# Latents in one pass, their norm ahead of the token scale, and softmax planes read later in a two-layer trunk

## The chip, the cores and the metric

The kernel runs on one core of a Trainium2 chip. The time is device microseconds of one execution. TensorE (PE in the profile) does the matrix products, ScalarE (ACT) and VectorE (DVE) the elementwise work, SyncE (SP) issues nearly all DMAs.

## The reference

Two pre-norm residual layers on 256 tokens of width 2048, fp32, 16 heads of 128. Layer a is multi-head latent attention: x is projected to a query latent (512), a key/value latent (256), one shared rotary key (64) and a gate (2048); both latents get an RMS norm of their own before they are projected up to the heads. Layer b is block attention, where 256 tokens are a single block, so it is causal attention with ALiBi. In both the output is multiplied with silu(gate) and projected back.

```python
h = rms_norm(x, g)                                   # per layer
proj = h @ w_in                                      # layer a
q_lat, kv_lat, k_rope, gate = proj[..., :512], proj[..., 512:768], proj[..., 768:832], proj[..., 832:]
q = rms_norm(q_lat) @ w_q_up;  kv = rms_norm(kv_lat) @ w_kv_up
o = causal_block_attention(q, k, v, 192 ** -0.5)     # q, k: 128 plain + 64 rotary, with QK norm
x = x + (o * silu(gate)) @ w_out_a
# layer b: q, k, v, gate from w_in_b, QK norm, ALiBi, x = x + (o * silu(gate)) @ w_out_b
```

## The kernel before

x is kept transposed (`xt`: 16 chunks of 128 features by 256 tokens). Each fp32 product is three TensorE matmuls of rounded parts: high times high, low times high, high times low. x is split by `split_x` (L331: ScalarE makes the high part, DVE the low one); a weight tile `W` is loaded by SP into `wr` (4 buffers), ScalarE makes `wh` (L147), DVE makes `wl` (L151). PSUM has 8 banks: five accumulators `acc` and three work banks.

The order of the program comes from `ordered(main, side)`: `main` is the list of matmul steps, `side` holds steps that become due some planner time after their `needs` (a step's lag, times 1.3). The result is run step by step; the matmuls are chained in that order, and each engine then works through its own instructions in the order given.

At the start, layer a's 832 latent columns are made in two passes over x, `lat0` and `lat1`, each 416 columns wide for 16 chunks. While `lat1` runs, the squares of x are summed; `token_scale` (L353) turns the sums into one factor per token: `ps_st` (a matmul with ones), three Newton rounds (`rsqrt`), and a step `g` that puts the root on a diagonal and spreads it by a matmul `ps_r`. `lat_out` copies the latents out of PSUM with that factor, `lat_norm` squares, norms and scales them; `lat_t` transposes them (`ps_lt`), for which TensorE has one and a half gate blocks (`gates[0]`, `gates[1][:HALF]`) to do meanwhile.

Then come eight groups of two heads (`group_a`): q_up and kv_up, then `turn`, and for each head `head_steps` (L450): s1 scores and softmax, s2 turns the probabilities by a DMA transpose between two byte-plane copies (`fly` on ScalarE and SP, then a copy of `pz` on DVE, L448) and splits them in `ph` (ScalarE) and `pl` (DVE, L491); s3 multiplies with v (`ps_o`) and writes `ohl`, the gated output. Between them stand the gate blocks.

The output projection `outs_a` has eight blocks of 256 columns. `out_done_a` adds a finished block to `xt`, splits it for layer b and sums its squares. A `reload` step brings `xt` back and at last the ALiBi table into `c_sb`; the first `alibi` bias (L883, ScalarE) reads it. The last projection `outs_b` ends with an add and a DMA to `outT` (L922).

## Time and profile before

| | |
|---|---|
| median of 3 runs | 754.15 us (752.91 to 754.26) |
| profiled execution | 752.38 us, span 750.6 us, mean TensorE clock 0.999 of full |
| TensorE busy | 740.6 us (99%) |
| DVE busy | 589.5 us (79%) |
| ScalarE busy | 491.3 us (65%) |
| DMA | 71.6% of 16 engines' span on SP's queue |

Busy is the time in which the engine has an instruction under way. Matmuls overlap in their pipeline, so an engine can be shown busy while a later one starts late; the distance from one start to the next says more. The bracket behind a timeline row tells the idle time in front of the instruction and what ended it.

### The profile page before, as it was taken

Reading aid. Unit: us, or ns where it says so; the run is one execution under the profiler, and the core shown is the slowest. Engines: PE = TensorE matmul, PEld = TensorE weight load, DVE = VectorE, ACT = ScalarE, POOL = GpSimd, SP = SyncE. Lnnn points to the kernel's source line nnn. Section 1 sums busy time; section 2 is a strip of 40 time slices with the busy share of each in tenths; the row PEclk is TensorE's granted clock in tenths of the full one; section 3 lists DMA queues with packets and bytes.
Section 4 is the critical chain, followed back from the end, with each engine's and each line's share of the span. In section 5 each row is a group of like instructions: output and inputs, shape, how many; then the busy total and the mean of one; then the engine's idle time right before and its main releaser. Section 6 shows DMA issues by size and latency. Waiting matters only on the chain.

```text
span 750.6 us, 13198 instructions
## 1 busy us (share of the span) xinstructions
PE 740.6 (99%) x4766; PEld 689.4 (92%) x4766; DVE 589.5 (79%) x1244; ACT 491.3 (65%) x1041; POOL 0.2 (0%) x4
## 2 busy tenths in 40 slices
PE   8999999999999999999999999999999999999997
PEld 7999999999999989988889988898889988899997
DVE  6978899999998696775788867887787967878563
ACT  7767888888877575555666666675666766565441
POOL 0000000000000000000000000000000000000000
PEclk9999999999999999999999999999999999999999
DMA  9866666666666966667787868877779778867761
GB/s 301 268 177 183 169 185 162 180 177 153 189 180 180 294 196 221 198 181 210 222 223 210 205 197 225 230 201 205 208 227 220 200 212 223 215 214 201 249 221 49
DMA packets 150258, 153.13 MB, mean 204 GB/s; under 512 B 47280, under 2 KB 119344, under 8 KB 150192
## 3 DMA queue, kind: packets, MB, share of 16 engines
q1 hardware_dynamic: 150048, 152.27, 71.6%
q8 instruction: 37, 0.61, 0.3%
q14 instruction: 29, 0.24, 0.1%
q10 hardware_dynamic: 144, 0.02, 0.0%
HBM read 139.68 MB, written 2.10 MB: 189 GB/s over the span
## 4 chain that ended last, share of the span: by engine, by line
PE 90%; DVE 5%; DMA 2%; ACT 1%; issue 1%; SPq 0%; DVEq 0%; ACTq 0%
PE acc L199 83%; PE ps_s L199 4%; DVE wl L151 3%; PE ps_o L199 2%; PE ps_ta L202 1%; DMA c_sb<-cst 1%; DMA wr<-w_in_a 1%; ACT wh L147 1%; DMA sm<-pz 0%; DVE xt L406 0%; ACT sq L598 0%; ACT sf L584 0%; DVE rs_y L328 0%; DVE rs_t L327 0%; PE ps_lt L202 0%
## 5 line engine op out<-in xcount | busy, mean ns | idle before, releaser
L147 ACT ACTIVATE wh<-wr 128x1024 fp32r<-128x1024 f32 (+3 forms) x265 | 288.4, 1092 | 143.1 <-PE acc L199 116.6
L151 DVE TENSOR_TENSOR wl<-wr,wh 128x1024 fp32r<-128x1024 f32 (+3 forms) x265 | 314.1, 1189 | 72.3 <-PE acc L199 41.8
L199 PE MATMUL acc<-wh,xhl 128*128 128x512 f32 (+1 forms) x896 | 265.6, 375 | 0.9 <-ACT wh L147 0.9
L199 PEld LDWEIGHTS acc<-wh,xhl 128*128 128x128 f32 x896 | 169.0, 190 | 21.7 <-ACT wh L147 1.5
L199 PE MATMUL acc<-xhl,wh 128*128 128x256 f32 (+1 forms) x768 | 173.4, 313 | 0.0
L199 PE MATMUL acc<-ohl,wh 128*128 128x256 f32 (+1 forms) x800 | 172.2, 307 | 0.0
L199 PE MATMUL acc<-wl,xhl 128*128 128x512 f32 (+1 forms) x448 | 167.8, 375 | 0.8 <-DVE wl L151 0.8
L199 PE MATMUL acc<-ohl,wl 128*128 128x256 f32 x512 | 140.7, 275 | 0.6 <-DVE wl L151 0.6
L199 PE MATMUL acc<-xhl,wl 128*128 128x256 f32 x512 | 140.3, 274 | 0.0
L199 PEld LDWEIGHTS acc<-ohl,wh 128*128 128x128 f32 x800 | 130.1, 191 | 6.0
L199 PEld LDWEIGHTS acc<-xhl,wh 128*128 128x128 f32 x768 | 126.5, 191 | 6.5
L199 PEld LDWEIGHTS acc<-ohl,wl 128*128 128x128 f32 x512 | 98.4, 192 | 1.3 <-DVE wl L151 1.2
L199 PEld LDWEIGHTS acc<-xhl,wl 128*128 128x128 f32 x512 | 98.4, 192 | 0.2
L199 PEld LDWEIGHTS acc<-wl,xhl 128*128 128x128 f32 x448 | 85.0, 190 | 11.6 <-DVE wl L151 1.6
L199 PE MATMUL acc<-wh,xt 128*128 128x384 f32 (+1 forms) x192 | 57.3, 356 | 0.0
L466 ACT ACTIVATE sm<-sm,mn 128x128 f32<-128x128 f32 x64 | 29.1, 457 | 12.9 <-DVE mn L464 12.9
L199 PEld LDWEIGHTS acc<-wh,xt 128*128 128x128 f32 x192 | 35.1, 190 | 1.2
L199 PE MATMUL acc<-wl,xt 128*128 128x384 f32 (+1 forms) x96 | 33.6, 350 | 1.5 <-DVE wl L151 1.5
L406 DVE TENSOR_TENSOR xt<-acc,xt 128x256 f32<-128x256 f32 (+1 forms) x37 | 16.1, 484 | 14.1 <-PE acc L199 14.1
L490 ACT CAST ph<-pz 128x256 fp32r<-128x256 f32 x32 | 12.9, 403 | 18.8 <-DVE pz L483 10.6
L507 DVE TENSOR_TENSOR ohl<-og,ohl 128x256 fp32r<-128x256 f32 x32 | 13.5, 424 | 12.2 <-ACT ohl L506 11.7
L506 ACT ACTIVATE ohl<-og 128x256 fp32r<-128x256 f32 x32 | 13.8, 433 | 12.8 <-DVE og L505 12.7
(150 smaller groups left out, 724.9 us busy)
## 6 DMA issues: line engine op xcount, KB each, us to landing
wr<-w_in_b SPq DMA_DIRECT2D x128, 512.0 KB, 4.0
wr<-w_in_a SPq DMA_DIRECT2D x32, 512.0 KB, 4.1
wr<-w_out_a SPq DMA_DIRECT2D x32, 512.0 KB, 4.5
wr<-w_out_b SPq DMA_DIRECT2D x32, 512.0 KB, 4.4
wr<-w_in_a SPq DMA_DIRECT2D x15, 416.0 KB, 5.0
wr<-w_q_up SPq DMA_DIRECT2D x16, 384.0 KB, 3.8
wr<-w_kv_up SPq DMA_DIRECT2D x8, 512.0 KB, 4.0
xt<-xT SPq DMA_DIRECT2D x4, 512.0 KB, 5.2
```

The lines of the kernel that those rows point to most:

```text
L147: nc.scalar.activation(self.ordering(self.h)[1], self.ordering(self.raw)[0], AF.Copy)
L151: nc.vector.tensor_tensor(self.ordering(self.l)[1], self.ordering(self.raw)[0], self.ordering(self.h.bitcast(F32))[1], op=ALU.subtract)
L199: chain(nc.tensor.matmul(*args, skip_group_check=True, **kw))
L202: chain(nc.tensor.transpose(*args))
L406: nc.vector.tensor_tensor(lines(y), unpaired(b[:, o:o + n]), lines(y), op=ALU.add)
L466: nc.scalar.activation(sm[:, sl], sm[:, sl], AF.Exp, bias=mn[:, t:t + 1], scale=-1.0, accum_out=rs[:, t:t + 1])
L490: nc.scalar.copy(ph, pz[:, :S])
L506: nc.scalar.activation(lines(ogh[:, h]), unpaired(og), AF.Copy)
L507: nc.vector.tensor_tensor(lines(ogl[:, h]), unpaired(og), lines(ogh[:, h].bitcast(F32)), op=ALU.subtract)
```

## The change

The latents are made in one pass: for each chunk of x both halves (832 columns) are multiplied, four accumulators are held, the x tiles are loaded in other places, and wl is used as the third of three products. The squares of x are summed in that pass. `lat_squares` takes the squares of the latents directly from PSUM; the tokens' factor enters through EPS (`lat_e`), and `normed` scales straight out of PSUM, one token half on ScalarE, the other on DVE. `token_scale` is three steps, its root and diagonal in one. `head_steps` of groups 1 to 5 gets `away=FLA`: `fly` early, the copy and the split (`s2_back`, L487 after) 1.3 × 4000 planner ns later. The output blocks, one gate block of layer b and the end of the last output block are reordered.

```diff
@@ -44,8 +44,8 @@
 
 
 
-PA, PB, LO, TU, TUB, S1, S2A, S2B, S3 = 9000, 6000, 5000, 3000, 10000, 4800, 6000, 9000, 3000
-FLB = 4500
+PA, PB, LO, TU, TUB, S1, S2A, S2B, S3 = 9000, 6000, 6000, 3000, 10000, 4800, 6000, 9000, 3000
+FLA, FLB = 4000, 4500
 SLACK = 1.3
 HOLD = 4500
 PACE, PACEB = 600, 3500
@@ -356,24 +356,28 @@
         def f():
             ps = work("ps_st")
             for t in range(2):
-                matmul(ps[:, t * P:(t + 1) * P], ssq[:, t * P:(t + 1) * P], ones, start=True, stop=True)
-            v = one.tile([P, 2], F32, name="rv_" + lay)
-            nc.vector.tensor_scalar(v, ps[:, :2 * P:P], 1.0 / DM, EPS, op0=ALU.mult, op1=ALU.add)
+                matmul(ps[:, t:t + 1], ssq[:, t * P:(t + 1) * P], ones[:, :1], start=True, stop=True)
+            v = out["v"] = one.tile([P, 2], F32, name="rv_" + lay)
+            nc.vector.tensor_scalar(v, ps[:, :2], 1.0 / DM, EPS, op0=ALU.mult, op1=ALU.add)
+
+        def h():
             r = out["r"] = one.tile([P, 2], F32, name="r_" + lay)
-            nc.vector.tensor_copy(r, rsqrt(v, 2, "x"))
+            d = out["diag"] = wk.tile([P, S], F32, tag="og", name="diag")
+            with tc.high_priority():
+                nc.vector.tensor_copy(r, rsqrt(out["v"], 2, "x"))
+                for t in range(2):
+                    nc.vector.tensor_scalar(d[:, t * P:(t + 1) * P], ident, r[:, t:t + 1], None, op0=ALU.mult)
             more()
 
         def g():
             pr = work("ps_r")
-            d = wk.tile([P, S], F32, tag="og", name="diag")
-            for t in range(2):
-                nc.vector.tensor_scalar(d[:, t * P:(t + 1) * P], ident, out["r"][:, t:t + 1], None, op0=ALU.mult)
-            matmul(pr[:, :S], ones, paired(d), start=True, stop=True)
+            matmul(pr[:, :S], ones, paired(out["diag"]), start=True, stop=True)
             rows = out["rows"] = one.tile([P, S], F32, tag="rr", name="rr_" + lay)
             nc.vector.tensor_copy(rows, pr[:, :S])
 
-        a = Step(f, 436, lag, needs, bank=True)
-        return a, Step(g, 436, 1500, [a], bank=True)
+        a = Step(f, 200, 800, needs, bank=True)
+        b = Step(h, 0, lag - 800, [a])
+        return a, b, Step(g, 436, 1500, [b], bank=True)
 
 
     gate_of = {}
@@ -540,7 +544,7 @@
         return Step(f, 0, 1000)
 
     def rest():
-        with tc.issue_after(lat1[0].w.dma):
+        with tc.issue_after(latent[7].w.dma):
             nc.sync.dma_start(g_sb[:, G_QN:G_END], gains[:, G_QN:])
             nc.sync.dma_start(c_sb, cst[:, :C_COS])
 
@@ -577,38 +581,70 @@
 
     lat_acc = []
 
-    def lat_out(i):
-        def f():
-            o = i * LAT // 2
-            for t in range(2):
-                nc.scalar.activation(lat[t][:, o:o + LAT // 2], lat_acc[i][t], AF.Copy, scale=scale_a["r"][:, t:t + 1])
-            if i:
-                lat_norm()
-        return f
-
     lat_st = {}
+    hf = LAT // 2
+
+    def blk_latents():
+
+
+        def go(wt, k, js):
+            if not lat_acc:
+                lat_acc.extend([acc("acc")[:, :hf] for _ in range(2)] for _ in range(2))
+            for i, j in enumerate(js):
+                ws = slice(i * hf, (i + 1) * hf)
+                wh, wl = paired(wt.h[:, 0, ws]), paired(wt.l[:, 0, ws])
+                for x, w, first, last in ((xh, wh, True, False), (xl, wh, False, False), (xh, wl, False, True)):
+                    for t in range(2):
+                        matmul(lat_acc[j][t], x[:, k, t * P:(t + 1) * P], w,
+                               start=k == 0 and first, stop=k == NC - 1 and last)
+
+        def step(k, js):
+            wt = W(w_in_a[k * P:(k + 1) * P, js[0] * hf:(js[-1] + 1) * hf], True)
+            return Step(lambda: go(wt, k, js), 6 * len(js) * 176, 0, w=wt)
+
+        return [step(0, (0,)), step(0, (1,))] + [step(k, (0, 1)) for k in range(1, NC)]
+
+
+    segments = ((0, 0, hf, 0, 0), (1, 0, QR - hf, hf, 0), (1, QR - hf, QR + KVR - hf, QR, 1), (1, QR + KVR - hf, hf, QR + KVR, 2))
+
+    def lat_squares():
+        with tc.high_priority():
+            squares_of()
+        tables()
+
+    def squares_of():
+        st = lat_st["st"] = one.tile([P, 2, 4], F32, name="lat_st")
+        for t in range(2):
+            for i, (j, lo, hi, _, _) in enumerate(segments):
+                sq = wk.tile([P, 512], F32, tag="gx", name="sq")
+                nc.scalar.activation(sq[:, :hi - lo], lat_acc[j][t][:, lo:hi], AF.Square, accum_out=st[:, t, i:i + 1])
 
     def lat_norm():
-        st = one.tile([P, 2, 3], F32, name="lat_st")
+        with tc.high_priority():
+            normed()
+
+    def normed():
+
+
+        st = lat_st["st"]
         v = one.tile([P, 2, 3], F32, name="lat_v")
-        parts = ((0, QR), (QR, KVR), (QR + KVR, ROPE))
-        for t in range(2):
-            for i, (o, n) in enumerate(parts):
-                sq = wk.tile([P, 512], F32, tag="gx", name="sq")
-                nc.scalar.activation(sq[:, :n], lat[t][:, o:o + n], AF.Square,
-                                     accum_out=st[:, t, i:i + 1])
...
+        ev = one.tile([P, 2], F32, name="lat_e")
+        nc.vector.tensor_scalar(ev, scale_a["v"], EPS, None, op0=ALU.mult)
+        nc.vector.tensor_tensor(st[:, :, 1], st[:, :, 0], st[:, :, 1], op=ALU.add)
+        for i, n in enumerate((QR, KVR, ROPE)):
+            nc.vector.scalar_tensor_tensor(v[:, :, i], st[:, :, i + 1], 1.0 / n, ev, op0=ALU.mult, op1=ALU.add)
         r = rsqrt(v.rearrange("p a b -> p (a b)"), 6, "l")
         krz = wk.tile([P, 384], F32, tag="sm", name="krz", bufs=3).rearrange("p (t a d) -> p t a d", t=2, a=3)
         nc.vector.memset(krz, 0.0)
         rp = wk.tile([P, 2, 1, ROPE], F32, tag="rp", name="rp", bufs=1)
...
+        for j, lo, hi, at, i in segments:
+            for t in range(2):
+                out = rp[:, t, 0] if i == 2 else lat[t][:, at:at + hi - lo]
+                by = r[:, 3 * t + i:3 * t + i + 1]
+                if t == 0:
+                    nc.scalar.activation(out, lat_acc[j][t][:, lo:hi], AF.Copy, scale=by)
+                else:
+                    nc.vector.tensor_scalar(out, lat_acc[j][t][:, lo:hi], by, None, op0=ALU.mult)
...
...
@@ -733,7 +768,7 @@
         for h in range(2):
             heads.append(head_steps(2 * g + h, scores(h), lambda: c_sb[:, C_MASK:C_MASK + 384],
                                     lambda h=h: [x[:, h] for x in z["v"]], 1090, turns + [kr], [], gates[g][-1:],
-                                    S2A, nc.scalar.copy))
+                                    S2A, nc.scalar.copy, away=FLA if 0 < g < 6 else 0))
         proj[0].needs += lats
         if g > 1:
             proj[-1].after += turns_of[-2]
@@ -745,22 +780,21 @@
         return proj
 
     pieces = [(0, 1), (1, 2), (2, 4), (4, 6), (6, 8), (8, 10), (10, 12), (12, 14), (14, 16)]
-    for i, (c0, c1) in enumerate(pieces):
-        main += [x_split(c0, c1)] + lat0[c0:c1]
-        for j in ((1, 2) if i == 0 else (i + 2,)):
-            if j < len(pieces):
-                lat0[pieces[j][0]].w.before = x_load(*pieces[j])
     squares = [Step(lambda j=j: sum_squares(ssq_a, 2 * j) or sum_squares(ssq_a, 2 * j + 1), 0, 2500) for j in range(4)]
-    main += lat1[:2] + [Step(rest)]
-    for j in range(4):
-        main += [squares[j]] + lat1[2 * j + 2:2 * j + 4]
-    main += lat1[10:] + gates[0] + gates[1][:HALF]
-    col_a, row_a = token_scale(ssq_a, "a", scale_a, squares, tables)
-    lo = [Step(lat_out(i), 0, LO, [col_a], b[-1:]) for i, b in enumerate((lat0, lat1))]
-    lo[1].after.append(lo[0])
-    lats = [Step(lat_t(b), 440, 2500, lo, bank=True) for b in range(3)]
+    main += [x_split(0, 1)] + latent[:2]
+    for i, (c0, c1) in enumerate(pieces[1:]):
+        latent[c0 + 1].w.before = x_load(c0, c1)
+        main += [x_split(c0, c1)] + [squares[j] for j in range(4) if c1 == (6, 10, 14, 16)[j]] + latent[c0 + 1:c1 + 1]
+        if c1 == 6:
+            main += [Step(rest)]
+    main += gates[0] + gates[1][:HALF]
+    col_a, r_a, row_a = token_scale(ssq_a, "a", scale_a, squares, lambda: None)
+    sq = Step(lat_squares, 0, 3000, latent[-1:])
+    lo = Step(lat_norm, 0, LO, [col_a, sq])
+    lo.after.append(r_a)
+    lats = [Step(lat_t(b), 440, 2500, [lo], bank=True) for b in range(3)]
     kr = Step(kr_t, 440, 2500, lats, bank=True)
-    side += [col_a, row_a] + lo + lats + [kr]
+    side += [col_a, r_a, sq, lo, row_a] + lats + [kr]
 
     def reload(j):
         def f():
@@ -814,9 +848,8 @@
             outs_a[2 * j][-1].needs.append(again)
     for b in outs_a[:4]:
         main += b[:12]
-    for b in outs_a[:4]:
-        main += b[12:]
-    main += sum(outs_a[4:], [])
+    o = outs_a
+    main += o[0][12:] + o[4][:8] + o[1][12:] + o[4][8:] + o[2][12:] + o[5][:8] + o[3][12:] + o[5][8:] + o[6] + o[7]
 
 
     x_b = x_a
@@ -911,6 +944,8 @@
         turns_of.extend([[tq], [tk]])
         side.extend([tq, tk])
         side.extend(s for h in hb[-4:] for s in h)
+        if g == 0:
+            gate = gate[:12] + gate[NC:NC + 4] + gate[12:NC] + gate[NC + 4:]
         return gate + q + k + v
 
     def out_done_b(c0, m):
@@ -918,6 +953,12 @@
             xt = res["x"]
             for b in range(0, len(a), m):
                 c = c0 + 2 * b // m
+                if c == NC - 2:
+                    for i, queue in enumerate((nc.sync, nc.scalar)):
+                        y = xt[:, c + i]
+                        nc.vector.tensor_tensor(lines(y), unpaired(a[b][:, i * S:(i + 1) * S]), lines(y), op=ALU.add)
+                        queue.dma_start(outT[(c + i) * P:(c + i + 1) * P], y)
+                    continue
                 added(a[b:b + m], xt, c)
                 nc.sync.dma_start(outT[c * P:(c + 2) * P].rearrange("(c p) t -> p c t", p=P), xt[:, c:c + 2])
         return f
@@ -925,8 +966,8 @@
     outs_b = [(blk_both if 8 <= c < 14 else blk_cols)(w_out_b[:, c * P:(c + n) * P], og, out_done_b(c, 2 if 8 <= c < 14 else 1))
               for c, n in ((0, 4), (4, 4), (8, 2), (10, 2), (12, 2), (14, 2))]
 
-    col_b, row_b = token_scale(ssq_b, "b", scale_b, [outs_a[7][-1]], scales_b, 7500)
-    side += [col_b, row_b]
+    col_b, r_b, row_b = token_scale(ssq_b, "b", scale_b, [outs_a[7][-1]], scales_b, 7500)
+    side += [col_b, r_b, row_b]
     hb = []
     for g in range(4):
         main += group_b(g)
```

DVE's order in the second group, before. `pz`, `pl` are planes of the heads, `gx` and `gate` the gate, `sr` the turned q and k, `wl` (128x1024) kv_up:

```order
L448 COPY pz<-sm 128x2x384
L151 TENSOR_TENSOR wl<-wr,wh 128x768
L491 TENSOR_TENSOR pl<-pz,ph 128x256
L394 TENSOR_TENSOR gx<-acc,rr_a 128x512
L151 TENSOR_TENSOR wl<-wr,wh 128x768
L448 COPY pz<-sm 128x2x384
L396 SCALAR_TENSOR_TENSOR gate<-gate,gx 128x512
L491 TENSOR_TENSOR pl<-pz,ph 128x256
L427 SCALAR_TENSOR_TENSOR sr_1704<-ps_ta,gq_a,sr_1704 128x256
L427 SCALAR_TENSOR_TENSOR sr_1704<-ps_ta,g_sb,sr_1704 128x512
L427 SCALAR_TENSOR_TENSOR sr_1704<-ps_ta,sr_1704 128x128
L151 TENSOR_TENSOR wl<-wr,wh 128x1024 x2
```

The same place after:

```order
L151 TENSOR_TENSOR wl<-wr,wh 128x768
L398 TENSOR_TENSOR gx<-acc,rr_a 128x512
L151 TENSOR_TENSOR wl<-wr,wh 128x768
L400 SCALAR_TENSOR_TENSOR gate<-gate,gx 128x512
L431 SCALAR_TENSOR_TENSOR sr_1695<-ps_ta,gq_a,sr_1695 128x256
L487 COPY pz<-sm 128x2x384
L431 SCALAR_TENSOR_TENSOR sr_1695<-ps_ta,g_sb,sr_1695 128x512
L495 TENSOR_TENSOR pl<-pz,ph 128x256
L431 SCALAR_TENSOR_TENSOR sr_1695<-ps_ta,sr_1695 128x128
L151 TENSOR_TENSOR wl<-wr,wh 128x1024
L487 COPY pz<-sm 128x2x384
L151 TENSOR_TENSOR wl<-wr,wh 128x1024
```

Both copies moved behind the gate; the second, and its `pl`, moved behind the first wl of kv_up.

DVE's order at layer b's token scale, before (`rs_y`, `rs_t`: the Newton rounds; `r_b`: the root; `diag`: what TensorE's `ps_r` reads):

```order
L326 TENSOR_TENSOR rs_t<-rv_b,rs_y 128x2
L327 SCALAR_TENSOR_TENSOR rs_t<-rs_t,rs_y 128x2
L328 SCALAR_TENSOR_TENSOR rs_y<-rs_t,rs_y 128x2
L363 COPY r_b<-rs_y 128x2
L151 TENSOR_TENSOR wl<-wr,wh 128x1024
L786 TENSOR_TENSOR rx_126<-r_b 128x2
L370 TENSOR_SCALAR diag<-c_sb,r_b 128x128
L787 TENSOR_SCALAR rx_126<-rx_126 128x2
L370 TENSOR_SCALAR diag<-c_sb,r_b 128x128
```

And after:

```order
L326 TENSOR_TENSOR rs_t<-rv_b,rs_y 128x2
L151 TENSOR_TENSOR wl<-wr,wh 128x1024
L327 SCALAR_TENSOR_TENSOR rs_t<-rs_t,rs_y 128x2
L328 SCALAR_TENSOR_TENSOR rs_y<-rs_t,rs_y 128x2
L367 COPY r_b<-rs_y 128x2
L369 TENSOR_SCALAR diag<-c_sb,r_b 128x128 x2
```

The wl that stood between root and diagonal now stands inside the last Newton round; root and diagonals follow each other.

ScalarE's order at the end of layer a's heads, before (`ohl`: the last two heads' outputs; `alibi`: the first bias of layer b, which reads the `c_sb` load):

```order
L147 ACTIVATE wh<-wr 128x1024 x2
L506 ACTIVATE ohl<-og 128x256
L147 ACTIVATE wh<-wr 128x1024
L506 ACTIVATE ohl<-og 128x256
L883 ACTIVATE alibi<-c_sb 128x384
L147 ACTIVATE wh<-wr 128x1024 x2
```

And after:

```order
L147 ACTIVATE wh<-wr 128x1024 x2
L510 ACTIVATE ohl<-og 128x256
L147 ACTIVATE wh<-wr 128x1024
L916 ACTIVATE alibi<-c_sb 128x384
L510 ACTIVATE ohl<-og 128x256
L147 ACTIVATE wh<-wr 128x1024
```

`alibi` moved in front of the last head's `ohl`.

## Rows read from the trace of the kernel before

**Rows 1.** Page, parts 1 and 4: busy time by engine, and the chain.
```profile
PE 740.6 (99%) x4766; PEld 689.4 (92%) x4766; DVE 589.5 (79%) x1244; ACT 491.3 (65%) x1041; POOL 0.2 (0%) x4
...
PE 90%; DVE 5%; DMA 2%; ACT 1%; issue 1%; SPq 0%; DVEq 0%; ACTq 0%
```

**Rows 2.** Windows: length, each engine's busy time (instructions), clock, DMA share, GB/s.
```profile
0.00:10.00 10.00, 7.26 (x47) 5.96 (x47) 4.57 (x10) 6.22 (x11) 0.20 (x4) 1.00 0.79 238
10.00:20.00 10.00, 9.85 (x54) 9.52 (x55) 9.08 (x16) 9.12 (x16) 0.00 (x0) 1.00 1.05 360
250.00:260.00 10.00, 10.00 (x92) 10.00 (x92) 5.81 (x9) 2.89 (x4) 0.00 (x0) 1.00 1.06 340
260.00:280.00 20.00, 19.40 (x134) 17.85 (x133) 18.13 (x31) 15.48 (x24) 0.00 (x0) 1.00 0.58 179
340.00:390.00 50.00, 50.00 (x234) 43.85 (x233) 35.09 (x60) 29.14 (x54) 0.00 (x0) 1.00 0.77 213
```

**Rows 3.** TensorE's waits, whole span: total us, times, longest.
```profile
PE acc L199 <- DVE wl L151: 2.9, 9, 0.6
...
PE acc L199 <- ACT wh L147: 0.9, 2, 0.6
PE ps_r L199 <- DVE diag L370: 0.5, 1, 0.5
PE ps_lt L202 <- DVE sf L608: 0.3, 1, 0.3
PE ps_s L199 <- DVE sr L427: 0.2, 1, 0.2
```

**Rows 4.** Timeline of TensorE, kv_up of a group: start, length.
```profile
123.97 0.46 PE L199 MATMUL acc<-wh,xt 128*128 128x512 f32 x1
124.70 0.48 PE L199 MATMUL acc<-wl,xt 128*128 128x512 f32 x1 [0.27 <-DVE wl L151]
```

**Rows 5.** Timelines of ScalarE and TensorE at the start.
```profile
6.12 0.58 ACT L147 ACTIVATE wh<-wr 128x416 fp32r<-128x416 f32 x1 [1.23 <-DMA wr<-w_in_a]
...
8.06 0.97 ACT L147 ACTIVATE wh<-wr 128x832 fp32r<-128x832 f32 x1 [0.34 <-DMA wr<-w_in_a]
...
10.14 0.44 PE L199 MATMUL acc<-wl,xhl 128*128 128x416 f32 x1 [0.62 <-DVE wl L151]
```

**Rows 6.** The chain of waits in the latents' norm: start, length.
```profile
45.64 0.73 ACT sq L598 x2
...
52.46 0.18 DVE rs_y L328
```

**Rows 7.** The chain of waits at layer b's token scale.
```profile
318.07 1.23 DVE wl L151
```

**Rows 8.** Timeline of DVE in front of the hole of rows 4.
```profile
121.42 0.42 DVE L491 TENSOR_TENSOR pl<-pz,ph 128x256 fp32r<-128x256 f32 x1
...
123.43 2.35 DVE L151 TENSOR_TENSOR wl<-wr,wh 128x1024 fp32r<-128x1024 f32 x2
```

**Rows 9.** DVE's waits, whole span, and its timeline at 232 us.
```profile
DVE pz L448 <- DMA sm<-pz: 4.2, 7, 1.4
...
232.02 0.61 DVE L448 COPY pz<-sm 128x768 uint16<-128x768 uint16 x1 [0.97 <-DMA sm<-pz]
```

**Rows 10.** Timelines of TensorE and ScalarE at layer a's last head.
```profile
252.95 0.39 PE L199 MATMUL ps_o<-p,v 128*128 128x128 f32 x2
...
256.10 0.43 ACT L506 ACTIVATE ohl<-og 128x256 fp32r<-128x256 f32 x1
260.02 0.52 ACT L883 ACTIVATE alibi<-c_sb 128x384 f32<-128x384 f32 x1 [3.49 <-DMA c_sb<-cst]
```

**Rows 11.** Timeline of the end, and a DMA issue (KB, us to landing).
```profile
746.73 0.69 DVE L406 TENSOR_TENSOR xt<-acc,xt 128x512 f32<-128x512 f32 x1 [6.76 <-PE acc L199]
747.45 0.38 SPq L922 DMA_DIRECT2D outT<-xt  x1
...
xt<-xT SPq DMA_DIRECT2D x2, 128.0 KB, 2.4
```

More of the change, by code (lines that the diff above doesn't have):

```diff
@@ L600, in lat_norm @@
-        for i, (o, n) in enumerate(parts):
-            nc.vector.tensor_scalar(v[:, :, i], st[:, :, i], 1.0 / n, EPS, op0=ALU.mult, op1=ALU.add)
+        ev = one.tile([P, 2], F32, name="lat_e")
[3 more added lines that the diff above has]
+            nc.vector.scalar_tensor_tensor(v[:, :, i], st[:, :, i + 1], 1.0 / n, ev, op0=ALU.mult, op1=ALU.add)
@@ L605, in lat_norm @@
         rp = wk.tile([P, 2, 1, ROPE], F32, tag="rp", name="rp", bufs=1)
-        for t in range(2):
-            for i, (o, n) in enumerate(parts[:2]):
-                nc.vector.tensor_scalar(lat[t][:, o:o + n], lat[t][:, o:o + n], r[:, 3 * t + i:3 * t + i + 1], None,
-                                        op0=ALU.mult)
-            o = parts[2][0]
-            nc.scalar.activation(rp[:, t, 0], lat[t][:, o:o + ROPE], AF.Copy, scale=r[:, 3 * t + 2:3 * t + 3])
+        for j, lo, hi, at, i in segments:
[6 more added lines that the diff above has]
+                    nc.vector.tensor_scalar(out, lat_acc[j][t][:, lo:hi], by, None, op0=ALU.mult)
         rope_of(rp, 2, 1, krz[:, :, 1:2])
@@ L645, in trunk @@
     rows_a = lambda: scale_a["rows"]
-    lat0 = blk_rows(w_in_a[:, 0:LAT // 2], x_a, lat_acc.append, 0, (1, 1))
-    lat1 = blk_rows(w_in_a[:, LAT // 2:LAT], x_a, lat_acc.append, 0)
+    latent = blk_latents()
     gates = [blk_cols(w_in_a[:, LAT + 256 * g:LAT + 256 * (g + 1)], x_a, gate_done(g, rows_a)) for g in range(8)]
```

## The prediction

> **What bounds the kernel now.** I read the page first. TensorE is busy for 99% of the span, and it is nine tenths of the chain that ended last [rows 1]. So the matmuls set the time, and the change leaves their number and widths alone (apart from eight small ones). It can gain only where TensorE stands still. I therefore read the windows for the steady rate: between 340 and 390 us there are 234 matmuls of 512 columns in 50 us, 0.214 us from start to start, without a hole [rows 2]. A matmul of 416 columns takes by the same rate 0.174 us. Only the start, 260 to 280 and a few spots show TensorE below full [rows 2].
>
> Next came the list of TensorE's waits: 2.9 us for wl in 9 places, 0.9 for wh, 0.5 for ps_r, 0.3 for ps_lt, 0.2 for ps_s [rows 3]. These are too small by themselves, and one hole shows by how much: a kv_up matmul starts at 123.97, the next, which needs wl, at 124.70 [rows 4]. That is 0.73 us for 0.214 of work, so 0.52 us are lost where the wait reads 0.27. I add 0.25 us to each wait for the refill of the pipe. With it about 4.8 us of waits in 14 places make 8.3 us; that and the tail is all there is to win.
>
> **The change part by part** (minus is faster).
>
> *Start.* ScalarE's wh conversions start when their tiles land: at 6.12 and 8.06 us [rows 5], with 672 and 1344 KB loaded (counted from the sizes in the loads' order). Before, 24 matmuls need 1344 KB, and wl is needed second: TensorE waits until 10.14 [rows 5], and that matmul and the ten behind it end near 12.1. After, the same 24 need 1088 KB (x0, two halves of w0, x1, w1), landing near 7.3 by a straight line between the two. wh costs 0.97 [rows 5], wl as long, so the fifth matmul of that row starts near 9.3, and eight at 0.174 end at 10.7. Gain 1.3. It is 0.4 if w1 lands as late as 8.06 with x1 and its own conversions in front, and at most 2.3, the 0.9 for wh [rows 3] and the 0.62 for wl [rows 5] with three refills. Behind it a row of 12 matmuls (2.1 us) needs 544 KB, 260 GB/s, and the queue has delivered 360 [rows 2]. **−1.3.**
>
> *Latents' norm.* The four scaled copies go, and the squares read PSUM before the token scale is known. In front of ps_lt lies a wait of 0.3 with its refill, 0.55. The new chain behind the last latent matmul is eight squares with their accumulator reads (one of 512 columns took 0.73 with its read [rows 6]; 1664 columns are 2.4 us in proportion and 5.8 if each costs as much, and I take 3.5), some 15 dependent small DVE steps of 0.2 (one has 0.18 [rows 6]), two wl in between at 1.23 [rows 7] and four pairs of outputs (1.5, taken as four times a 256-column pass of 0.42 [rows 8]): about 10.5 us. One and a half gate blocks are 144 matmuls of 256 columns at 0.109, 15.7 us, of cover, of which some 12.6 stand in front of the first transposes in the new order. So about 2 us of slack; without that cover each late microsecond is lost, and the four latent banks also come free later for the gate blocks. Range −0.9 to +1.6. **−0.6.**
>
> *Token scale.* ps_st becomes one column wide, at most 0.2 for eight matmuls. In layer b DVE runs a wl of 1.23 us between the root and the diagonal [rows 7], and TensorE's ps_r waits 0.5 behind it [rows 3]. Afterwards the root and both diagonals stand together, as the second order listing shows, and the wl that they pass is one that TensorE wants later (the wl buffers run ahead there). **−0.8 with refill**, 0 if that wl is missed at once.
>
> *Planes read later.* In five places of layer a the first wl of kv_up is late, because DVE works off two plane copies and pl (0.42 [rows 8]) in front of it; the two wl then take 2.35 us together [rows 8]. For groups 1 to 5 the copies now follow the gate, and the second stands behind the first wl (first order listing). Heads 2 to 9 lie under four of the five holes; the first hole (heads of group 0) stays. Per hole one copy (0.61 [rows 9]) and one pl (0.42) leave the front, 1.0 us against 0.52 lost: the hole closes. What is late next is ps_o of the second head, whose pl now ends about when ps_o wants it. 4 × 0.52 = **−2.1**, between −0.4 and −2.6. At 232 us DVE stood 0.97 us for a transpose [rows 9], and ps_s waited 0.2 for it; the heads of that spot come about 2 us later in the new order: **−0.45.**
>
> *Output blocks of layer a.* Between 260 and 280 TensorE idles 0.6 us in two holes [rows 2], 1.1 with refills, where the add, the split and the squares of one block stand in front of a wl. The new order sets halves of blocks 4 and 5 between the ends of 0 to 3, so they lie apart. New is that the second bank of block 4 waits for the add of block 0, which I put at 0.55. **−0.55.**
>
> *The ALiBi load.* This one goes the other way. ScalarE stood 3.49 us at `alibi` for the load of c_sb, which came at 260.02 [rows 10]. That cost nothing, because the last head's `ohl` was done at 256.1 [rows 10]. Now `alibi` stands in front of that `ohl` (third order listing), and o0[12:] wants head 15 at about 257.1 on the old clock: the last ps_o pair starts at 252.95 [rows 10], and 36 matmuls of 256 columns at 0.109 (92 in 10 us [rows 2]) lie between; the order keeps the number of matmuls in front of that place. `alibi` 0.52, `ohl` 0.43 [rows 10] and its low part, taken as 0.43 too, leave c_sb until 255.7. The DMA rings run at 1.06 and 340 GB/s there [rows 2], and c_sb keeps its place behind the same bytes, though the x tiles ahead of it go out somewhat earlier. Landing between 255 and 260.0: from 0 to 4.3 us lost. I take 257.2, a little under the middle, for the earlier x tiles: **+1.5.**
>
> *Tail.* The last add takes 0.69 us for two chunks, and its 256 KB go out at 747.45 and end the span at 750.6, 3.15 us later [rows 11]. Now a half is added in about 0.42 (a DVE pass of 256 columns [rows 8]) and the other ends some 0.32 behind it, each with a DMA of its own; 128 KB take 2.4 [rows 11]. The end is 746.73 + 0.74 + 2.4 = 749.9. **−0.7**, from 0 to −1. The Trainium skill, "DMA: Bandwidth & Descriptors", section "Anatomy of one DMA", gives a transfer 2.0 us fixed plus its bytes at 436 GB/s; an estimate by that page is 2.6 and 2.3 us, so the smaller piece would save 0.3 and not 0.75. The same page ("Issuing engines are not separate DMA queues") has the two queues share 16 engines, which speaks against a gain from the second queue. The trace has the larger price for 256 KB (3.15), so I keep it; by the page the sum would be 0.4 smaller.
>
> The interleaved gate blocks of layer b and the moved constant loads I cost at nothing: behind ps_r TensorE has no hole in layer b to win [rows 2, 3], and its weight tiles stand four deep.
>
> **Sum:** −1.3 −0.6 −0.1 −0.8 −2.1 −0.45 −0.55 +1.5 −0.7 = −5.1 us. The profiled execution took 752.38 us (span 750.6, 1.8 around it), 1.8 below the median of 754.15. Against its own time the sum gives 747.3. The terms are differences, and a new set of runs is compared by its median, so I set them there: **749.0 us.** 0.2% or 1.5 us is about what a measurement of this kernel can tell from no change.
>
> **The rivals.**
> 1. *The ALiBi load takes most back.* c_sb lands at 260 as before: 4.3 us lost instead of 1.5. Result 751.8. For it: rings at 340 GB/s and the unchanged place in the queue. Against it: earlier x tiles. Chance 0.2.
> 2. *DVE is the bound of layer a.* The planes' work is moved, not removed; holes reappear at ps_o behind the late pl. Then planes and output blocks give 0.5 instead of 2.65: 751.2. For it: DVE carries two wl in a row for 2.35 us next to the stall [rows 8]. Against it: it has idle time, waiting for transposes 4.2 us in 7 places [rows 9]. Chance 0.15.
> 3. *Slower: the early-issued transposes come late.* The plane copies now stand in front of `sr` and the second wl in five groups. If a transpose has not landed, DVE stops with both behind it, as at 232. Each of ten copies 0.97 late would lose 9.7 us against 2.1 expected, and the time would be 754.15 − 5.1 + 2.1 + 9.7 = about 761. It decides from 0.3 us per copy (then the other gains, 3.0, are gone), and 0.45 make it slower by 0.2%. For it: copies that waited so far did so for 0.6 us on average [rows 9]. Against it: only 7 did, and the planner now sets the copy 1.3 × 4000 ns behind the issue of its transpose, where it had none between them. Chance 0.05.
> 4. *The reordering does not do what it says:* the start stays bound by the transfers, the norm by ScalarE's queue, and only ps_r, the tail and part of the planes are won, about 2.5 us less the ALiBi's 1.5: 753.2. Chance 0.1.
>
> My forecast has 0.5. The range from 746.0 (no ALiBi loss and the upper ends of start and planes) to 752.4 takes in rivals 1 and 2. Faster by over 0.2% (below 752.6): forecast, rivals 1 and 2, 0.85; same: rival 4, 0.10; slower: rival 3, 0.05.
>
> **What would show it.** TensorE's waits after: wl from 9 places to about 4, no ps_r and no ps_lt; 24 matmuls done before 11 us; ScalarE's wait at `alibi` followed by a TensorE wait for `ohl`; the last two DMAs out before 747.6. Wrong would make it: new TensorE waits for pl in groups 1 to 5, for a bank around the end of the latents, or an idle of over 4 us at the end of the first output blocks.

## The result and the profile after

The changed kernel took 758.66 us (median of 9 runs) beside 754.15 of the kernel before (9 runs): ratio 1.0055 [1.0037, 1.0072], so it is slower by some 0.55%. One of the changed kernel's nine runs took 961.22 us at a mean granted clock of 0.754; the ratio leaves it out. The profiled execution took 759.02 us with a span of 757.2, 6.6 us above that of before. The forecast was 749.0, and slower had a chance of 0.05.

The page says little: TensorE's share fell from 99 to 98% [rows 1].

```profile
PE 743.2 (98%) x4766; PEld 692.1 (91%) x4766; DVE 587.8 (78%) x1247; ACT 489.8 (65%) x1043; POOL 0.2 (0%) x4
```

TensorE's waits, in the columns of [rows 3], say what changed. The nine waits for wl have become two, and ps_r and ps_lt are gone. Four names are new or larger: `ohl`, `ph`, `wh`, `pl`.

```profile
PE acc L199 <- ACT ohl L510: 2.9, 1, 2.9
PE ps_o L199 <- ACT ph L494: 2.4, 2, 1.6
PE acc L199 <- ACT wh L147: 1.8, 1, 1.8
...
PE ps_o L199 <- DVE pl L495: 1.1, 2, 0.6
PE acc L199 <- DVE wl L151: 0.5, 2, 0.4
```

The waits cannot give the whole 6.6 us, so I went through the starts. For each TensorE matmul I took the time to the next start and subtracted the distance that a matmul of its width has where nothing is late (0.216 us for 512 columns, 0.109 for 256, 0.11 for narrower ones, 0.27 for `ps_r`). What is left above zero is called lost, and it is summed by stretch; "by starts" below means this sum. It gives 26.6 us lost before and 33.2 after:

```
stretch, us     before  after   difference   what stands there
0 to 20          3.5     3.4     -0.1        first tiles
40 to 60         1.5     0.8     -0.8        latents' norm
80 to 100        1.0     1.4     +0.4
100 to 200       8.0     6.1     -1.8        kv_up of the head groups
200 to 220       1.0     4.1     +3.1        heads 10, 11
220 to 240       1.9     2.9     +1.0        heads 12, 13
240 to 260       0.7     3.8     +3.1        wait for ohl
260 to 280       1.4     4.1     +2.7        granted clock
300 to 340       1.3     0.6     -0.7        token scale of layer b
```

**The ALiBi load.** The timeline of TensorE shows the place that the third order listing pointed to: a standstill of 3.13 us from start to start, for work of 0.11, behind the last head's `ohl`.

```profile
259.09 0.28 PE L199 MATMUL acc<-ohl,wl 128*128 128x256 f32 x1
262.22 1.04 PE L199 MATMUL acc<-ohl,wh 128*128 128x256 f32 x2 [2.85 <-ACT ohl L510]
263.91 0.63 PE L199 MATMUL acc<-ohl,wh 128*128 128x512 f32 x1
264.34 0.42 PE L199 MATMUL acc<-ohl,wl 128*128 128x256 f32 x1
```

On ScalarE `alibi` waits for c_sb, and `ohl` stands behind it. The load of c_sb is issued on SP at 254.93 and lands 6.4 us later.

```profile
261.33 0.52 ACT L916 ACTIVATE alibi<-c_sb 128x384 f32<-128x384 f32 x1 [2.28 <-DMA c_sb<-cst]
261.76 0.41 ACT L510 ACTIVATE ohl<-og 128x256 fp32r<-128x256 f32 x1
...
254.93 0.50 SPq L802 DMA_DIRECT2D c_sb<-cst  x1
```

But the loss does not end there. In the windows (columns as in [rows 2]) the granted clock stands at 1.00 until 262 and then falls to 0.50, which is the 1.2 GHz level, although TensorE works again from 262.22 on. In the timeline above, the 512 columns at 263.91 take 0.43 us to the next start, where [rows 2] had 0.214.

```profile
258.00:260.00 2.00, 1.37 (x13) 1.18 (x11) 0.40 (x2) 1.05 (x1) 0.00 (x0) 1.00 1.08 353
260.00:262.00 2.00, 0.00 (x0) 0.00 (x0) 0.00 (x0) 0.67 (x2) 0.00 (x0) 1.00 1.09 350
262.00:264.00 2.00, 1.70 (x7) 1.51 (x8) 0.43 (x1) 0.18 (x2) 0.00 (x0) 0.62 0.11 35
264.00:266.00 2.00, 1.86 (x6) 1.26 (x6) 1.85 (x3) 2.00 (x4) 0.00 (x0) 0.50 0.00 0
266.00:268.00 2.00, 2.00 (x7) 1.69 (x7) 1.10 (x3) 0.36 (x1) 0.00 (x0) 0.50 0.39 114
268.00:270.00 2.00, 2.00 (x10) 1.72 (x9) 0.37 (x1) 0.43 (x1) 0.00 (x0) 0.68 0.43 148
```

The missing shares of the last four windows (0.38, 0.5, 0.5 and 0.32 of 2 us) make 3.4 us, which is 6.8 us at half speed. With the standstill's 3.0 that is 6.4.

**The late planes.** In group 5 the second copy now stands behind both wl of kv_up. First DVE and ScalarE (`ph`, the last row), then TensorE:

```profile
206.95 0.60 DVE L487 COPY pz<-sm 128x768 uint16<-128x768 uint16 x1
207.44 1.21 DVE L151 TENSOR_TENSOR wl<-wr,wh 128x1024 fp32r<-128x1024 f32 x1
208.56 0.42 DVE L495 TENSOR_TENSOR pl<-pz,ph 128x256 fp32r<-128x256 f32 x1
...
209.41 1.22 DVE L151 TENSOR_TENSOR wl<-wr,wh 128x1024 fp32r<-128x1024 f32 x1
...
211.21 0.59 DVE L487 COPY pz<-sm 128x768 uint16<-128x768 uint16 x1
...
212.39 0.41 ACT L494 CAST ph<-pz 128x256 fp32r<-128x256 f32 x1
```

```profile
209.03 0.38 PE L199 MATMUL ps_o<-pl,vh 128*128 128x256 f32 x1 [0.56 <-DVE pl L495]
212.85 0.38 PE L199 MATMUL ps_o<-ph,vh 128*128 128x256 f32 x1 [1.59 <-ACT ph L494]
```

At heads 12 and 13, whose copies were not moved, the transpose is issued on SP behind three weight loads, and DVE waits 2.51 us for it (0.97 before [rows 9]); ps_o is late twice.

```profile
225.09 3.68 SPq L133 DMA_DIRECT2D wr<-w_out_a  x3
228.82 1.52 SPq L446 DMA_TRANSPOSE sm<-pz  x1
...
234.37 0.60 DVE L452 COPY pz<-sm 128x768 uint16<-128x768 uint16 x1 [2.51 <-DMA sm<-pz]
...
235.51 0.38 PE L199 MATMUL ps_o<-ph,vh 128*128 128x256 f32 x1 [0.83 <-ACT ph L494]
236.46 0.38 PE L199 MATMUL ps_o<-pl,vh 128*128 128x256 f32 x1 [0.57 <-DVE pl L495]
```

**Start and tail.** The second chunk's wh starts at 8.79 in this execution, where I had its tile at 7.3. At the end the two halves go out on two queues; the issue list gives 128 KB 1.7 and 1.8 us, from the start of the issue to the landing, and 2.9 as the median of the seven stores of 256 KB in front of them. The last store of before, the only one between 745 and 751 us, took 2.2 (the last line, from the kernel before).

```profile
8.79 0.95 ACT L147 ACTIVATE wh<-wr 128x832 fp32r<-128x832 f32 x1 [2.36 <-DMA wr<-w_in_a]
...
753.57 0.76 DVE L959 TENSOR_TENSOR xt<-acc,xt 128x256 f32<-128x256 f32 x2 [6.76 <-PE acc L199]
754.02 0.36 SPq L960 DMA_DIRECT2D outT<-xt  x1
754.36 0.35 ACTq L960 DMA_DIRECT2D outT<-xt  x1
```

```profile
outT<-xt SPq DMA_DIRECT2D x7, 256.0 KB, 2.9
...
outT<-xt ACTq DMA_DIRECT2D x1, 128.0 KB, 1.8
...
outT<-xt SPq DMA_DIRECT2D x1, 256.0 KB, 2.2
```

### The profile page after: what moved, and what is told of

Read it like the earlier page. It is cut to its first block, busy times and chain, and to the rows that moved or that the text cites. A ratio compares the mean times of both kernels' runs of the same rounds, so it can differ in the third digit from the quotient of the medians.

```text
span 757.2 us, 13210 instructions
## 1 busy us (share of the span) xinstructions
PE 743.2 (98%) x4766; PEld 692.1 (91%) x4766; DVE 587.8 (78%) x1247; ACT 489.8 (65%) x1043; POOL 0.2 (0%) x4
## 4 chain that ended last, share of the span: by engine, by line
PE 65%; DVE 0%; DVEq 0%; issue 0%
PE acc L199 62%; PE ps_s L199 1%; PE ps_o L199 1%; DVE xt L410 0%; PE ps_r L199 0%; DVE ohl L511 0%; DVE xt L959 0%; PE ps_st L199 0%; DVEq L1036 0%
## 5 line engine op out<-in xcount | busy, mean ns | idle before, releaser
L199 PE MATMUL acc<-wh,xhl 128*128 128x512 f32 (+1 forms) x896 | 260.0, 375 | 1.8 <-ACT wh L147 1.8
L199 PE MATMUL acc<-ohl,wh 128*128 128x256 f32 (+1 forms) x800 | 175.3, 310 | 3.1 <-ACT ohl L510 2.9
L199 PE MATMUL acc<-wl,xhl 128*128 128x512 f32 (+1 forms) x448 | 162.2, 374 | 0.1
L199 PE MATMUL acc<-wl,xt 128*128 128x384 f32 (+1 forms) x96 | 33.2, 346 | 0.5 <-DVE wl L151 0.5
L494 ACT CAST ph<-pz 128x256 fp32r<-128x256 f32 x32 | 12.9, 403 | 23.3 <-DVE pz L487 12.5
```

The lines of the kernel that those rows point to most:

```text
L199: chain(nc.tensor.matmul(*args, skip_group_check=True, **kw))
L494: nc.scalar.copy(ph, pz[:, :S])
```

## Experiments

Each was timed beside the kernel before on the same chip; "before" is the median of that kernel there. The ratios, with their 95% intervals, compare better from one chip to another than the medians do. Line numbers in diffs are left out. All start from the changed kernel.

### The ALiBi load: alibi and csb_early

**alibi** puts the first `alibi` behind the last `ohl` on ScalarE. That one swap is all that its built order shows.

```diff
-            nc.scalar.activation(lines(ogh[:, h]), unpaired(og), AF.Copy)
+            res["ohl"] = nc.scalar.activation(lines(ogh[:, h]), unpaired(og), AF.Copy)
...
+                if h == 0:
+                    after(i, res["ohl"])
```

> The changed kernel with one pair of rows swapped on ScalarE: the first alibi behind the last head's ohl. Theory A (the 2.9 us wait of TensorE for ohl, and the half clock granted from 262 to 269 us, both come from alibi standing in front): both go, 3.0 + 3.4 us, median near 752.3. Theory B (the clock falls there for another reason): only the wait goes, near 755.6, and the windows 262 to 269 still show a granted clock of 0.5. Theory C (c_sb's place was no more than a symptom of late heads): under 1 us, near 758.

Measured: 753.31 (before 753.4), ratio 0.9994 [0.998, 1.0008], span 750.7. The wait for `ohl` is gone and so is the half clock, as the windows show:

```profile
258.00:260.00 2.00, 1.87 (x12) 1.24 (x10) 0.67 (x2) 0.38 (x2) 0.00 (x0) 1.00 1.08 353
260.00:270.00 10.00, 9.54 (x66) 8.97 (x66) 6.85 (x9) 6.46 (x10) 0.00 (x0) 1.00 0.62 203
```

By starts, 240 to 280 loses 2.2 us instead of 7.9. So the swap costs 5.7, a little less than 6.4: the wait of block 4's second bank (0.5 for `xt` here) was hidden in the standstill. Against the ratio of the changed kernel (1.0055) the swap gives 0.61% back, some 4.6 us. The half clock is no accident of one execution: the mean granted clock was 0.993 to 0.997 in the eight runs of the changed kernel's ratio and is 0.998 to 1.000 in all twelve of alibi.

**csb_early** leaves `alibi` in front (seven of ScalarE's instructions earlier still) and loads c_sb ahead of the x tiles.

```diff
-    for j in range(5):
+    for j in (4, 0, 1, 2, 3):
```

> The changed kernel with the ALiBi table loaded in front of the four x tiles instead of behind them; alibi stays in front of the last ohl on ScalarE. Theory (the price of alibi's place is the landing of c_sb): the 2.9 us wait for ohl and the half clock go, median near 752.3 to 753.3, like the kernel alibi (753.3). Rival (something else delays that ohl): the wait stays over 1.5 us, above 756.

Measured: 752.99 (before 752.6), ratio 1.0007 [0.9993, 1.0022], span 750.3, no wait for `ohl`, clock 1.00. ScalarE does `ohl` at 257.47:

```profile
257.47 0.42 ACT L510 ACTIVATE ohl<-og 128x256 fp32r<-128x256 f32 x1
```

So it is the landing of c_sb that is paid for, and the order matters only because of it. Against the changed kernel's ratio this is 0.48%, some 3.6 us.

### The half clock: fill, stall and stall_fill

**fill** adds 48 useless 128x128 bf16 matmuls to the changed kernel, in front of the matmuls that wait for `ohl`.

```diff
-    main += o[0][12:] + o[4][:8] + ...
+    main += o[0][12:15] + [Step(fill)] + o[0][15:] + o[4][:8] + ...
```

> The changed kernel with 48 small matmuls without use put in front of the first matmul that waits for the last ohl; the wait itself stays. Theory A (the clock falls because TensorE stands still for 3 us): granted clock 1.0 throughout, 3.4 us of half speed gone, median near 755.3, the wait still there. Theory B (it falls for another reason): granted clock still 0.5 for some us, median 758.7 or above.

Measured: 757.18 (before 753.4), ratio 1.0039 [1.0022, 1.0055], span 755.1. The place keeps its clock, but now the half clock stands at 212 to 215, behind the hole of group 5:

```profile
256.00:266.00 10.00, 9.26 (x95) 8.41 (x94) 5.22 (x9) 4.27 (x7) 0.00 (x0) 1.00 0.63 201
...
212.00:215.00 3.00, 3.00 (x11) 2.46 (x12) 1.26 (x5) 1.74 (x11) 0.00 (x0) 0.57 0.07 24
```

The mean granted clock of its eight runs is 0.998 to 1.000. But two things are mixed in its profile, so it decides little. The next two have no holes in group 5. **stall** is off_out2 (below) with 11 useless ScalarE copies in front of the last `ohl`; **stall_fill** adds the 48 matmuls to it.

```diff
+                late += [nc.scalar.activation(scr, og, AF.Copy) for _ in range(11)]
```

> The kernel off_out2 (748.7, alibi behind ohl, granted clock 1.0) with eleven copies without use on ScalarE in front of the last head's ohl: TensorE stands still for 3 to 4 us at the same matmul, with no load involved. Theory (standing still brings half clock behind it): 3.5 for the wait and about 3 for the clock, near 755, with granted clock 0.5 for several us behind the wait. Rival (the clock fell for another reason): wait alone, near 752.2, clock 1.0.

> The kernel stall with 48 small matmuls without use in front of the matmul that waits. Theory: the wait costs the same 3.5 us, but the clock stays at 1.0 there: near 752.2, some 3 us below stall. Rival: the same time as stall.

Measured: stall 757.03 (before 754.36), ratio 1.004 [1.0026, 1.0053], span 753.7; stall_fill 755.05, ratio 1.0027 [1.0009, 1.0044], span 751.9. In stall TensorE stands 4.6 us for `ohl`, and windows of 0.68 and 0.50 follow, then 0.97:

```profile
258.00:260.00 2.00, 0.00 (x0) 0.00 (x0) 0.00 (x0) 1.87 (x5) 0.00 (x0) 1.00 0.82 264
260.00:262.00 2.00, 1.13 (x4) 0.96 (x5) 0.42 (x1) 1.20 (x4) 0.00 (x0) 0.68 0.05 15
262.00:264.00 2.00, 2.00 (x11) 2.00 (x11) 1.20 (x2) 1.41 (x3) 0.00 (x0) 0.50 0.00 0
264.00:266.00 2.00, 2.00 (x20) 2.00 (x19) 1.75 (x4) 0.97 (x3) 0.00 (x0) 0.97 0.09 22
```

The missing shares make 1.7 us, half of what the clock cost in the changed kernel. By the ratios stall is 0.86% above off_out2 (0.9954), some 6.5 us, and the wait and the clock together make 6.3.

In stall_fill the same place keeps 1.00, with useless work in it and a wait of 1.7 left:

```profile
256.00:258.00 2.00, 1.52 (x28) 1.34 (x25) 0.00 (x0) 1.86 (x5) 0.00 (x0) 1.00 1.06 340
258.00:260.00 2.00, 0.67 (x3) 0.48 (x4) 0.43 (x1) 1.56 (x4) 0.00 (x0) 1.00 0.18 58
260.00:262.00 2.00, 2.00 (x20) 2.00 (x20) 1.43 (x2) 1.54 (x3) 0.00 (x0) 1.00 0.03 8
```

Useless matmuls end no wait for `ohl`: from the last useful matmul in front of it to the first behind it there are 4.9 us in stall and 4.7 in stall_fill, from start to start. The median fell by 2.0 us all the same. The intervals of the two ratios overlap, so the times alone show little; the clocks show more. The mean granted clock was 0.995 to 0.997 in all twelve runs of stall and 0.998 to 1.000 in eleven of the twelve of stall_fill (0.995 in the other). By starts 240 to 280 lost 7.3 us in stall; in stall_fill it lost 3.0, and the 48 matmuls took 2.7, so 1.5 us were kept there. What the useless work kept is the clock. The Trainium skill, "TensorE: Matmul & The Clock Gate", section "HAM oscillation — how this bites in real kernels", says that a TensorE left waiting falls back to the slow clock and starts the next work there. The windows agree: in stall the clock is down in the one in which work resumes (0.68, at 260.87), in the changed kernel it falls in the one in which work has just resumed (0.62).

### The late planes: fla4, planes_off and planes_g6

**fla4** moves the copies in groups 1 to 4 alone. In its built order `alibi` falls behind `ohl` by itself, and from group 5 on the order differs on all engines, so it is not a change of the copies alone.

```diff
-  S2A, nc.scalar.copy, away=FLA if 0 < g < 6 else 0))
+  S2A, nc.scalar.copy, away=FLA if 0 < g < 5 else 0))
```

> The changed kernel with late planes for groups 1 to 4 only; in its built order the first alibi stands behind the last ohl too. Theory A: the holes of group 5's heads (ps_o at 208 to 213 us, 2.9 us) go, and with alibi behind ohl the wait and the half clock as well (6.4 us); the transposes near 234 us may still be late (1.8 us): median near 749.5. Rival (holes of the last groups come from transposes behind the output weights, not from late planes): holes of the same size stay between 205 and 240, median near 752.5.

Measured: 750.34 (before 753.4), ratio 0.9954 [0.9937, 0.9972], span 748.1, clock 1.00. No wait for `ph` or `pl` is left, but DVE's copy at 231.94 waits 1.73 us for its transpose with `sr` behind it, and TensorE waits for `sr`:

```profile
PE ps_s L199 <- DVE sr L431: 1.5, 1, 1.5
...
PE ps_o L199 <- DVE sr L431: 0.8, 1, 0.8
```

**planes_off** has `away=0` everywhere, with alibi's edit.

> The changed kernel with no late planes in layer a, alibi behind the last ohl. Theory (late planes close four holes of 0.52 us in groups 1 to 4 and are worth 2 us there): 2 us above the kernel fla4 (750.3), near 752.4, and TensorE waits for wl again in five places. Rival (the holes closed in groups 1 to 4 come back as other waits): near 750.3.

Measured: 749.96 (before 753.77), ratio 0.9951 [0.9932, 0.997], span 748.7. The holes at wl are back, and the time is that of fla4. The longest of them, 1.3, is not one of the old holes alone: it stands behind a copy that waited 1.92 us for its transpose at 186.74, where off_out2 (below), the same program up to there, waited 0.23.

```profile
PE acc L199 <- DVE wl L151: 2.4, 5, 1.3
```

So late planes in four groups are worth nothing together. By starts fla4 loses 4.4 us at 120 to 200 and planes_off 7.9; four other kernels with the same program there lose 6.2 to 6.7, so the usual gain is 1.8 to 2.3. At 200 to 240 fla4 loses 1.7 and 1.1 us more than planes_off. The first of the two stands in group 5, the first group whose copies are in front again: they waited 0.34 and 0.66 us for their transposes (one of them 1.81 in fla4_outs and 2.05 in fla4_two, below), with `sr` and wl behind them. In planes_off they did not wait. There the group's two transposes were issued 5.6 us apart, at 200.37 and 205.97, and landed after 3.8 and 2.8 us; in fla4 1.9 us apart, at 197.46 and 199.35, and after 4.4 and 5.3.

**planes_g6** has late planes in groups 1 to 4 and 6 (heads 12 and 13), with alibi's edit, to take the copy at 231.94 out of the way of `sr`.

> Late planes for groups 1 to 4 and 6. In fla4 the copy of group 6's first head stops DVE for 1.73 us until its transpose lands, with sr behind it, and TensorE loses 1.7 us at ps_s. Theory (the wait is only in the wrong place): the copy goes behind sr, the hole closes, 1.5 us below fla4, near 748.8. Rival (the transpose is what is late): the hole moves to ps_o of the same head, near 750.3.

Measured: 751.12 (before 753.77), ratio 0.9968 [0.995, 0.9985], span 750.2. The hole moved on to ps_o, as the rival said:

```profile
234.62 0.38 PE L199 MATMUL ps_o<-ph,vh 128*128 128x256 f32 x1 [0.90 <-ACT ph L494]
```

### The start: two_pass, fla4_two and off_split

**two_pass** and **fla4_two** are the changed kernel and fla4 with the two passes and the load order of before; fla4_two has alibi's edit.

```diff
-    latent = blk_latents()
+    lat0 = blk_rows(w_in_a[:, 0:hf], x_a, lat_acc.append, 0, (1, 1))
+    lat1 = blk_rows(w_in_a[:, hf:LAT], x_a, lat_acc.append, 0)
```

> The changed kernel with the latents in two passes over x as before, all else as changed (norm from PSUM, planes, alibi in front). Theory (one pass gained nothing at the start, 3.0 us lost in the first 10 us in both): median within 1 us of 758.7. Rival (my forecast's term, one pass gains 1.3 us): near 760.

> The kernel fla4 with the latents in two passes over x. Theory (one pass is worth about 1.2 us at the start when its third weight tile lands early, as in three of four profiles): near 751.5. Rival (nothing, as the changed kernel's own profile and two_pass say): near 750.3.

Measured: two_pass 758.09 (before 753.4), ratio 1.0065 [1.004, 1.009], the same as the changed kernel within the intervals. This pair does not price the start: in the profile of two_pass the half clock behind `ohl` cost 1.7 us (0.81, 0.50 and 0.84 in the windows of 2 us from 262 to 268), half of what it cost in the changed kernel's. fla4_two 752.88 (before 753.77), ratio 0.9999 [0.9983, 1.0014], 0.45% above fla4. Some of it is not the start: the hole at 208 us is larger there (a wait of 1.31 for wl, 0.37 in fla4). So I set the losses of the first 20 us by starts beside each other. With two passes they are 3.5 (before), 3.9 and 3.6 us. In the ten kernels that share the changed kernel's start (stall and stall_fill left out) they are 1.9 to 3.4, 2.5 in the mean, and the changed kernel's own 3.4 is the largest. One pass gains 1.2 us in the mean, from one profile of each kernel. The tile that I had at 7.3 is converted between 7.16 and 8.79 in these ten.

**off_split** is planes_off with the second chunk's weight tile in two halves of 208 KB.

```diff
-  return [step(0, (0,)), step(0, (1,))] + [step(k, (0, 1)) for k in range(1, NC)]
+  return [step(k, (j,)) for k in range(2) for j in range(2)] + [step(k, (0, 1)) for k in range(2, NC)]
```

> The kernel planes_off with the second chunk's weight tile of the latents loaded as two halves of 208 KB. In planes_off TensorE waits 1.2 us at 7 us for that tile of 416 KB. Theory (the loads issued behind it share the rings with it, so half a tile lands earlier): that hole shrinks to 0.5, median near 749.3. Rival (the bytes in front of the 24 matmuls are the same, nothing gained; one more conversion each on ScalarE and DVE): near 750.

Measured: 749.68 (before 752.6), ratio 0.997 [0.9958, 0.9981]; planes_off had 0.9951. The first 20 us lose 2.0 us against 2.2: no difference to be told.

### The output blocks: fla4_outs and off_out2

**fla4_outs** is fla4 with the output order of before and alibi's edit. **off_out2** is planes_off with the ends of blocks 0 and 1 in front of block 4, whose second bank waits for the add of block 0.

```diff
-    main += o[0][12:] + o[4][:8] + o[1][12:] + o[4][8:] + o[2][12:] + o[5][:8] + ...
+    main += o[0][12:] + o[1][12:] + o[4][:8] + o[2][12:] + o[4][8:] + o[5][:8] + ...
```

> The kernel fla4 with layer a's output blocks in the order of before. Theory (the new order removes two holes of 0.57 us each and makes one of 0.62): 0.5 us above fla4, near 750.8, with two TensorE waits for wl near 265 us. Rival (the old order is no worse): at or below 750.3.

> The kernel planes_off (750.0) with one pair of pieces of layer a's output order swapped, so that block 4 begins after the end of block 1 instead of block 0. Theory (the 0.62 us hole at 257 us is block 4's second bank waiting for the add of block 0, and the add is done one piece later): hole gone, near 749.4. Rival (the add is late by more than a piece, or wl becomes late next): near 750.

Measured: fla4_outs 751.95 (before 753.77), ratio 0.997 [0.9954, 0.9986]. Its two holes in front of wl at 269 and 272 are back, but its profiled execution has a half clock at 213 to 215 too, so the 0.16% to fla4 is not the order's alone. off_out2 748.69 (before 752.6), ratio 0.9954 [0.9942, 0.9967]: the wait for `xt` is gone, and 240 to 260 loses 0.6 us instead of 1.3. The ratio is that of planes_off (0.9951), so the gain is seen in the trace and not in the times.

### The best version: fla3_out2 and fla3_split

Late planes in groups 1 to 3 alone (`0 < g < 4`), alibi's edit and off_out2's order; **fla3_split** adds off_split's halves.

> Late planes in groups 1 to 3 alone, alibi behind the last ohl, output order as in off_out2. Theory (each group with late planes only hands its 0.5 us to the first group without): three holes gone, one of about 1.5 to 2 us in the heads of group 4 or 5: within 0.7 us of off_out2. Rival (late planes gain as long as a gate block follows, and groups 5 and 6 alone lose): 1.5 us below off_out2, near 748.

> The kernel fla3_out2 (747.8) with the second chunk's weight tile in two halves, as in off_split, whose start lost 1.3 us instead of 2.2 in the first 10 us and 0.7 more in the next ten. Expected: 0 to 0.7 us below fla3_out2, 747.1 to 747.8; rival (the extra conversions cost as much): at or above 747.8.

Measured: fla3_out2 747.83 (before 752.6), ratio 0.9945 [0.993, 0.996], span 745.3. fla3_split 747.5 (before 754.36), ratio 0.9911 [0.9896, 0.9926], span 746.0. The two medians can't be told apart; the ratios differ mostly by the kernel before, which came out 1.8 us apart. fla3_out2 is 0.9 us below off_out2, between what its theory and its rival said, and the intervals overlap. Both kernels beat the kernel before and the changed one. In fla3_out2 TensorE's waits behind the warm-up are down to these:

```profile
PE acc L199 <- ACT wh L147: 0.7, 1, 0.7
PE acc L199 <- DVE wl L151: 0.5, 2, 0.4
PE acc L199 <- DVE xt L667: 0.2, 1, 0.2
```

## Why the prediction was wrong

**The ALiBi load (+1.5, 0 to 4.3)** is the step that failed most. Place and mechanism were as written, and the standstill of 3.0 us lies in its range. What the step left out is what the standstill does to the clock: 3.4 us more at 0.50. Together 6.4, beyond the upper end; alibi and csb_early took 5.7 and 5.9 of it back (240 to 280, by starts) by different means. Rival 1 had the load alone (751.8) and so missed it too.

It was not the only one. Between the sum (−5.1) and this execution (+6.6) lie 11.7 us. By starts 4.8 of them stand at 240 to 280 (+5.75, where the load and the output blocks were put at +0.95 together), 3.4 at 100 to 220 (+1.3 for −2.1, the planes), 1.5 at 232, 1.2 at the start and 0.5 at the tail. With the load's place put right, alibi (753.31) still lies above the range's upper end of 752.4.

**Planes read later (−2.1)** failed in its second half. The holes of groups 1 to 4 closed (−1.8 at 100 to 200). "What is late next is ps_o of the second head" was written down and then priced at nothing. New waits for `pl` in groups 1 to 5, which the prediction named as a sign of being wrong, came at 209.03. The late ps_o cost 2.9 us in group 5 by starts (0.8 at 208, 1.75 at 211, 0.35 at 213). This is rival 2, priced at 2.15, with one difference: it does not return in every group. fla4 and planes_off have the same time, and fla3_out2 loses 1.4 us less than off_out2 at 120 to 180 without giving it back: groups 1 to 3 keep their gain by starts (fla3_split shows the same 3.1 us at 120 to 180), the fourth and fifth do not. Behind the fourth it is the transposes of group 5 that land late (fla4); in the fifth itself no copy waited for a transpose, and the second copy simply stands behind both wl. That the last groups have fewer gate blocks behind them as cover is argued only.

**232 us (−0.45)** had the wrong sign: +1.0. The transpose at 228.82 is issued behind three weight loads and DVE waited 2.51 us for it. In the kernel before it was issued behind one, at 228.68, and the copy ran at 232.02. That the heads come later did not help, since the transpose came later still.

**The other terms.** The start's −1.3 holds in the mean (1.2 over ten kernels), and not in this execution (−0.1), because the tile came 1.5 us later than my straight line; the 24 matmuls, wanted before 11 us, were done near 12.5 (12.3 before). The norm's −0.6 came as −0.8 here; in six of the other 13 kernels without a stall 40 to 60 us is as low (0.70 to 0.78), in seven it is not (1.2 to 1.7), so the gain over all 14 is 0.45 in the mean. The token scale's −0.8 came as −0.7. The −0.1 for ps_st came to nothing: from start to start the four matmuls of one column took 0.36 us, as the four of 128 columns had before. The output blocks: both old holes left and the new one of block 4 came, 0.5 by its wait in alibi where I had 0.55; off_out2 removes it. The tail's −0.7 came as −0.24: from the start of the last add to the span's end 3.87 us before [rows 11] and 3.63 after. The sum took a landing for the end of the span: it set 2.4 for 128 KB against 3.15 for 256 KB, but of the 3.15 only 2.2 are the store's, and some 1.0 lies between its landing and the end. That 1.0 is there after the change too. The Trainium skill, "DMA: Bandwidth & Descriptors", section "Anatomy of one DMA", gives 2.6 and 2.3 us for the two sizes as an estimate. That section speaks of DMAs that GpSimd issues, and here SyncE and ScalarE issue them; the stores took 2.2 and 1.8, less than the estimate, with a difference of 0.4 that is near its 0.3.

**Rival 3**, the only slower one, was not what happened: none of the ten moved copies waited for its transpose. Its mechanism, a copy that waits with `sr` and wl behind it, came in fla4 and planes_g6 (see the late planes above). With the ALiBi load and the late planes of groups 4 and 5 taken out and one pair of output pieces swapped, fla3_out2 is 5.2 us faster by starts. My sum without the ALiBi term was −6.6.

**Open.** At 207 to 212 us the half clock follows a hole of 1.6 us in the profile of fill, and holes of 1.1 and 0.8 us in that of fla4_outs. The same hole of 1.6 us is not followed by it in the changed kernel, alibi and csb_early; no run here tells why. Why the half clock behind `ohl` lasted 6.8 us in the changed kernel and 3.4 in stall and two_pass is open too. The last DMA landed near 756.1 (754.36 and 1.8 from the start of its issue), and what fills the 1.0 us to the span's end the rows do not show.
